# The second layer's memory keys and values, made at the end of the recurrent layer instead of at the start

## The chip, the cores and the metric

The kernel runs on one core of one Trainium2 chip, in one launch. The metric is device time in microseconds (us), the median of several runs. Each run can also be recorded by the hardware profiler; every line of the profile below comes from one such execution of the kernel before. Engines: PE is TensorE (PEld its weight loads), DVE VectorE, ACT ScalarE, POOL GpSimd, SP SyncE, which here only issues transfers.

## The reference, cut to what matters

Two layers over 512 frames of width 1024. Layer 0 mixes by a recurrence (12 heads of 64) and, beside it, by attention into 256 memory tokens (4 heads); layer 1 by chunked attention and, beside it, by memory attention with its own keys and values of the same normalised memory.

```python
def memory_attention(q_mem, mem_n, w_mem_kv):
    k_m, v_m = jnp.split(mem_n @ w_mem_kv, 2, axis=-1)
    ...
    s = jnp.einsum('bshd,bmhd->bhsm', q, k).astype(jnp.float32) * HEAD_DIM ** -0.5
    p = jax.nn.softmax(s, axis=-1).astype(v.dtype)
    return jnp.einsum('bhsm,bmhd->bshd', p, v).reshape(bsz, seq, D_MEMQ)

mem_n = rms_norm(mem, mem_norm)
for layer in range(DEPTH):
    h = rms_norm(x, ln1[layer])
    ...
    mo = memory_attention(q_mem, mem_n, w_mem_kv[layer])
    x = x + jnp.concatenate([mix, mo], axis=-1) @ w_out[layer]
    x = x + conv_glu(rms_norm(x, ln2[layer]), ffn_in[layer], ffn_conv[layer],
                     ffn_conv_b[layer], ffn_out[layer])
return rms_norm(x, ln_f)
```

The keys and values of layer 1 depend on the memory and on the weights alone, so they may be made anywhere ahead of layer 1's attention.

## The kernel before, in words

Everything is fp32 with the features on the partitions. A product is split: each operand into a rounded high half and a low half (`fp32r`), and `dense` does three matmuls per block of 128 features: high by high (L198), high by the activation's low (L199), and, after all of those, the weight's low by high (L202). A weight is loaded by SP into one of two `wraw` buffers, ACT casts it to its high half (L169), and the low half is made either by DVE (L175) or, where `lo_on` is set (the recurrent part), by an ACT copy with the sign turned (L172) on which a POOL transfer adds the weight once more from memory.

The order of the work in the program's text is made by `weave`: each piece of work is a generator that yields planned costs; the one that is furthest behind its share goes next, a pair `(cost, wait)` holds it back in planned time, and a callable holds it until a condition is true. A scheduler then gives each engine its own queue, worked off in order: an instruction that waits holds up all behind it.

The recurrent layer goes by six pairs of heads. `prepare` makes a pair's projections, decays and norms; `front` makes its chunk products and solves a triangular system of 31 dependent steps on DVE (L661 to L668; its right side comes and its result `Xs` goes through memory: `Lr<-d`, `d<-Xs` at L671, `Tt<-d` at L674); `back` turns the solve's result `Tt` into products (transposes L775 on DVE; L780, L788, L794, L804, L815, L821 on PE, ACT's copies between), runs the recurrence over eight chunks (L835 on PE, L836 on DVE, L840 on PE, seven dependent steps), normalises y (L549, a root in small DVE steps, L558), and scales it (L856 to L867).

Before the first pairs, one `weave` interleaves `prepare(0)` with `mem_kv`, which makes keys and values of both layers (L518 the keys' scaling, L528 to L530 the values' three matmuls) and stores the second layer's in `kv1`. The memory is split by `scaled_split` (L238 on ACT, L239 on DVE; in the start's own copy L475 and L476), its norm stands in `macc`. The last `weave` holds `back` of pair 4, `front` and `back` of pair 5, a chain of the layer's memory queries (`q_mem`, L878), the mixed tiles fetched back (`flush_mix`) and the memory attention `mA` (scores L921, maxima L269, exponentials L273, sums' reciprocal L275, division L278, turns L286, values L296), and `ahead`, which starts two tiles of the output projection. After it the x tiles are loaded (L951) and `out_proj` adds them (L333).

Of the kernel before, what the change touches and what calls it, by code (L numbers as in the profile page):

```python
# [111 lines left out]
def trunk_kernel(ctx, tc, A, out):  # L112
# [211 lines left out]
    def out_proj(l, act, gain, h_, l_, xT, order, pre=(), done=()):  # L324
        for m in range(KD):
# [7 lines left out]
            V.tensor_tensor(xT[:, m], xT[:, m], ps[:], op=ALU.add)  # L333
# [106 lines left out]
    mrc = lp.tile([P, 4], F32, name="mrc")  # L440

# [69 lines left out]
    def mem_kv():  # L511
        for l in range(2):
            km, vm_ = (kmT0, vm0) if l == 0 else (tmp(F32, (P, 2, 256)) for _ in range(2))
            for f in range(2):
                w = load_w(A["w_memk"][l, f])
                ps = ps_l()
                yield from dense(ps[:, :NMEM], [(w, K8)], pair_of(mh, ml))
                V.tensor_tensor(km[:, f], ps[:, :NMEM], macc[:, NMEM:], op=ALU.mult)  # L518
            ps = [ps_l(), ps_l()]
            for u in range(2):  # L520
                wh, wl = load_w(A["w_memv"][l, u])
                for j in range(4):
                    k = u * 4 + j
                    for t in range(2):
                        ws = slice(j * 256, (j + 1) * 256)
                        ts = slice(t * P, (t + 1) * P)
                        pt = ps[t][:, :256]
                        PE.matmul(pt, mh[:, k, ts], wh[:, ws], start=k == 0, stop=False)  # L528
                        PE.matmul(pt, ml[:, k, ts], wh[:, ws], start=False, stop=False)
                        PE.matmul(pt, mh[:, k, ts], wl[:, ws], start=False, stop=k == 7)  # L530
                    yield 650
            for t in range(2):
                SC.activation(vm_[:, t], ps[t][:, :256], AF.Copy, scale=mrc[:, t:t + 1])
            if l:
                nc.sync.dma_start(kv1[0], km)
                nc.sync.dma_start(kv1[1], vm_)

    MEMKV_COST = 2 * (16 * 648 + 8 * 650) + 600
# [228 lines left out]
    def back(i, T, dst, tiles=own_tiles, go=None):  # L767
# [57 lines left out]

        psc = bank((P, 8, 64))
# [45 lines left out]

    def q_mem(src, act, qm):
# [53 lines left out]
    def told(g, n):  # L927
        yield from g
        over.add(n)

    def ahead():
        yield lambda: "mem" in over and "state" in Ts[NPAIR - 1]
        yield from out_ahead(0, act1, AHEAD, 2, pre)

# [342 lines left out]
```

## Time and profile before

| | us |
|---|---|
| median of 3 runs | 1379.11 (1378.86 to 1379.75) |
| profiled execution, its own time | 1377.77 |
| span in that profile | 1376.0 |
| mean granted TensorE clock | 0.987 |
| PE busy | 1319.7 (96% of the span) |
| DVE busy | 826.9 (60%) |
| ACT busy | 611.6 (44%) |
| POOL busy | 34.1 (2%) |

A row of the timeline has the start, the length, the engine, the line of the code, the operation with what it writes and reads, and in brackets the idle time of the engine ahead of it with what ended it. Consecutive like instructions share a row (x9). A row of windows gives the stretch and its length, then each engine's busy time with its count in brackets, then the granted clock, the transfers' share and GB/s. A row of groups has the busy time, the mean length of one in ns, and the idle time ahead of them.

### The profile page before, as it was taken

How to read it: one execution, taken by the hardware profiler on the slowest of the kernel's cores; microseconds unless marked ns; L12 is line 12 of the kernel's file. 1: busy time of each engine (PE TensorE's matmuls, PEld its weight loads, DVE VectorE, ACT ScalarE, POOL GpSimd, SP SyncE). 2: the span in 40 equal slices, each digit the busy share in tenths (PEclk: the TensorE clock that was granted, in tenths of full speed). 3: DMA queues.
4: the chain of work that ended last, by engine and by line, in shares of the span. 5: the costliest groups of instructions: out<-in, count | busy, mean ns of one | idle time of the engine just before them, and what ended most of it. 6: DMA issues, size and time to landing. Idle time of an engine off the chain costs nothing. (4 is left out here: it accounts for less than half of the span.)

```text
span 1376.0 us, 20868 instructions
## 1 busy us (share of the span) xinstructions
PE 1319.7 (96%) x8266; PEld 1071.2 (78%) x8266; DVE 826.9 (60%) x1752; ACT 611.6 (44%) x1022; POOL 34.1 (2%) x55
## 2 busy tenths in 40 slices
PE   6999999995999999999999999999999999999996
PEld 5777777774688888888888878786788888888886
DVE  7876789774666555565333667657665565563324
ACT  5556555552444333333222566657443333332321
POOL 3000000000000000000000000000000000000000
PEclk9999999997999999999999999999999999999998
DMA  5276544451042223223232422223223222222332
GB/s 181 83 208 136 109 108 110 99 142 42 24 146 92 92 94 106 92 93 102 84 98 85 152 91 74 90 92 99 93 92 103 96 93 102 98 88 85 104 94 75
DMA packets 63506, 139.18 MB, mean 101 GB/s; under 512 B 24624, under 2 KB 28336, under 8 KB 63408
## 3 DMA queue, kind: packets, MB, share of 16 engines
q1 hardware_dynamic: 60672, 127.89, 29.3%
q0 software_dynamic: 2736, 9.96, 4.2%
q8 instruction: 65, 1.06, 0.3%
q14 instruction: 33, 0.27, 0.1%
HBM read 131.01 MB, written 6.82 MB: 100 GB/s over the span
## 5 line engine op out<-in xcount | busy, mean ns | idle before, releaser
L175 DVE TENSOR_TENSOR wlo<-wraw,whi 128x1024 fp32r<-128x1024 f32 x183 | 218.9, 1197 | 128.4 <-PE psd L202 118.3
L169 ACT CAST whi<-wraw 128x1024 fp32r<-128x1024 f32 (+1 forms) x202 | 207.6, 1029 | 153.3 <-PE psd L199 38.5
L198 PE MATMUL psd<-r1h,whi 128*128 128x512 f32 x336 | 136.6, 407 | 1.3 <-ACT whi L169 1.2
L198 PE MATMUL psf<-r2h,whi 128*128 128x512 f32 x352 | 137.2, 390 | 0.0
L198 PE MATMUL psf<-r1h,whi 128*128 128x512 f32 x352 | 137.2, 390 | 0.0
L199 PE MATMUL psf<-r1l,whi 128*128 128x512 f32 x352 | 137.1, 390 | 0.0
L199 PE MATMUL psf<-r2l,whi 128*128 128x512 f32 x352 | 137.1, 390 | 0.0
L199 PE MATMUL psd<-r1l,whi 128*128 128x512 f32 x336 | 134.1, 399 | 0.0
L202 PE MATMUL psd<-r1h,wlo 128*128 128x512 f32 x336 | 92.5, 403 | 3.1 <-DMA wlo<-in_wA_dram 3.1
L199 PE MATMUL psd<-f3l,whi 128*128 128x512 f32 (+1 forms) x238 | 88.7, 377 | 0.0
L198 PE MATMUL psd<-f3h,whi 128*128 128x512 f32 (+1 forms) x238 | 88.6, 377 | 0.0
L358 DVE TENSOR_TENSOR tmp<-psf,rho 128x512 f32<-128x512 f32 x44 | 30.4, 692 | 94.7 <-PE psf L202 94.7
L202 PE MATMUL psf<-r1h,wlo 128*128 128x512 f32 x352 | 87.0, 389 | 0.0
L202 PE MATMUL psf<-r2h,wlo 128*128 128x512 f32 x352 | 86.9, 389 | 0.0
L198 PE MATMUL psd<-r2h,whi 128*128 128x512 f32 (+1 forms) x200 | 77.6, 392 | 0.1
L198 PEld LDWEIGHTS psd<-r1h,whi 128*128 128x128 f32 x336 | 63.8, 190 | 17.4 <-issue 2.4
L199 PE MATMUL psd<-r2l,whi 128*128 128x512 f32 (+1 forms) x200 | 76.4, 385 | 0.8 <-DVE r2l L215 0.8
L202 PEld LDWEIGHTS psf<-r1h,wlo 128*128 128x128 f32 x352 | 66.1, 188 | 13.7
L202 PEld LDWEIGHTS psf<-r2h,wlo 128*128 128x128 f32 x352 | 66.1, 188 | 13.7
L199 PEld LDWEIGHTS psf<-r1l,whi 128*128 128x128 f32 x352 | 66.1, 188 | 13.6
L198 PEld LDWEIGHTS psf<-r2h,whi 128*128 128x128 f32 x352 | 66.1, 188 | 13.7
L199 PEld LDWEIGHTS psf<-r2l,whi 128*128 128x128 f32 x352 | 66.1, 188 | 13.6
(352 smaller groups left out, 2429.2 us busy)
## 6 DMA issues: line engine op xcount, KB each, us to landing
wraw<-in_ffn_in_dram SPq DMA_DIRECT2D x88, 512.0 KB, 3.3
wraw<-in_ffn_out_dram SPq DMA_DIRECT2D x32, 448.0 KB, 3.3
wraw<-in_wA_dram SPq DMA_DIRECT2D x20, 512.0 KB, 4.3
wlo<-in_wA_dram POOLq DMA_DIRECT2D x17, 512.0 KB, 7.7
wraw<-in_w_out_dram SPq DMA_DIRECT2D x16, 512.0 KB, 3.8
wraw<-in_ffn_out_dram SPq DMA_DIRECT2D x16, 512.0 KB, 4.1
wraw<-in_wB_dram SPq DMA_DIRECT2D x8, 512.0 KB, 3.4
Lr<-d SPq DMA_DIRECT2D x24, 128.0 KB, 5.5
```

The source lines that it names most:

```text
L169: SC.copy(hi[:, :n], raw)
L175: V.tensor_tensor(lo[:, :n], raw, hi[:, :n], op=ALU.subtract)
L198: PE.matmul(ps, wh[:, j * P:(j + 1) * P], ah, start=start and n == 0, stop=False)
L199: PE.matmul(ps, wh[:, j * P:(j + 1) * P], al, start=False, stop=False)
L202: PE.matmul(ps, wl[:, j * P:(j + 1) * P], act(k)[0], start=False, stop=stop and n == len(ks) - 1)
L358: V.tensor_tensor(v[:], pv[:], rho[:], op=ALU.mult)
```

## The change

`mem_kv` now makes one layer per call, in banks that are passed in, with weights requested one ahead, the values' high products first and low ones after, and smaller planned costs. The first `weave` makes layer 0 alone. In the last `weave` a new chain does the memory queries, then `mem_again`, then `flush_mix`: `mem_again` loads the memory once more through the two `wraw` buffers, splits it into tiles of `r1h` and `r1l` that `flush_mix` fills later, and calls `mem_kv(1, ...)`, with the low halves by POOL. The memory attention has its own place in the `weave`, from the queries on. The last pair's `back` holds its recurrence until "kv" is in `over`; between its `front` and `back` a planned wait of 25000 ns is put. `ahead` loads two x tiles into a `wraw` buffer, and `out_proj` adds them from there. Line numbers in the changed file are 11 higher in the recurrent part, 13 in the later part of `back`, 15 to 17 in the memory's.

```diff
-    def out_proj(l, act, gain, h_, l_, xT, order, pre=(), done=()):
+    def out_proj(l, act, gain, h_, l_, xT, order, pre=(), done=(), early=None):
...
-            V.tensor_tensor(xT[:, m], xT[:, m], ps[:], op=ALU.add)
+            was = early[:, m * S:(m + 1) * S] if early is not None and m < 2 else xT[:, m]
+            V.tensor_tensor(xT[:, m], was, ps[:], op=ALU.add)
...
+    mrho = lp.tile([P, NMEM], F32, name="mrho")
...
-    def mem_kv():
-        for l in range(2):
-            km, vm_ = (kmT0, vm0) if l == 0 else (tmp(F32, (P, 2, 256)) for _ in range(2))
-            for f in range(2):
-                w = load_w(A["w_memk"][l, f])
-                ps = ps_l()
-                yield from dense(ps[:, :NMEM], [(w, K8)], pair_of(mh, ml))
-                V.tensor_tensor(km[:, f], ps[:, :NMEM], macc[:, NMEM:], op=ALU.mult)
...
-    MEMKV_COST = 2 * (16 * 648 + 8 * 650) + 600
+    def mem_kv(l, mh, ml, mrho, bank):
+        km, vm_ = (kmT0, vm0) if l == 0 else (tmp(F32, (P, 2, 256)) for _ in range(2))
+        srcs = [A["w_memk"][l, 0], A["w_memk"][l, 1], A["w_memv"][l, 0], A["w_memv"][l, 1]]
+        sent = [load_w(srcs.pop(0))]
+
+        def take_w():
+            if srcs:
+                sent.append(load_w(srcs.pop(0)))
+            return sent.pop(0)
+
+        for f in range(2):
+            w = take_w()
+            ps = bank()
+            for y in dense(ps[:, :NMEM], [(w, K8)], pair_of(mh, ml)):
+                yield y / 2
+            V.tensor_tensor(km[:, f], ps[:, :NMEM], mrho, op=ALU.mult)
+        ps = [bank(), bank()]
+        for u in range(2):
+            wh, wl = take_w()
...
+            for k, t, ws, ts in at:
+                PE.matmul(ps[t][:, :256], mh[:, k, ts], wh[:, ws], start=k == 0, stop=False)
+                PE.matmul(ps[t][:, :256], ml[:, k, ts], wh[:, ws], start=False, stop=False)
+                if t:
+                    yield 480
+            for k, t, ws, ts in at:
+                PE.matmul(ps[t][:, :256], mh[:, k, ts], wl[:, ws], start=False, stop=k == 7)
+                if t:
+                    yield 240
...
+    MEMKV_COST = 8 * 648 + 8 * 720
...
+        if go is not None:
+            yield lambda: "kv" in over
         psc = bank((P, 8, 64))
         psy = bank((P, 8, 64))
...
-    weave([(first, .981 * PREP_COST), (chain(lora_one(), mem_kv()), 16 * 648 + MEMKV_COST)])
+    V.tensor_copy(mrho[:], macc[:, NMEM:])
+    weave([(first, .981 * PREP_COST), (chain(lora_one(), mem_kv(0, mh, ml, mrho[:], ps_l)), 16 * 648 + MEMKV_COST)])
...
+    def q_there():
+        yield lambda: "q" in over
+
+    def later(ns):
+        yield 0, ns
...
-        yield lambda: "mem" in over and "state" in Ts[NPAIR - 1]
+        yield lambda: "mem" in over and "flush" in over and "state" in Ts[NPAIR - 1]
         yield from out_ahead(0, act1, AHEAD, 2, pre)
+        early.append(wp.tile([P, 1024], F32, name="wraw", tag="wraw", bufs=2))
+        nc.sync.dma_start(early[0][:], A["xT"][:, 0:2].rearrange("p a b -> p (a b)"))
...
+    def mem_again():
+        h4, l4 = (t[:, 0:4].rearrange("p a (b m) -> p (a b) m", b=2) for t in (r1h, r1l))
+        for u in range(2):
+            raw = wp.tile([P, 1024], F32, name="wraw", tag="wraw", bufs=2)
+            nc.sync.dma_start(raw[:], A["memT"][:, 4 * u:4 * u + 4].rearrange("p a b -> p (a b)"))
+            for j in range(4):
+                scaled_split(raw[:, j * NMEM:(j + 1) * NMEM], 4 * u + j, "mem_norm", h4, l4)
+        yield 0, 2000
+        yield from mem_kv(1, h4, l4, mrho[:], ps_d)
+        over.add("kv")
     a_, b_ = NPAIR - 2, NPAIR - 1
     weave([(told(back(a_, Ts[a_], dst_mix), "back"), 1.5 * BACK_COST),
-           (chain(front(b_, Ts[b_]), back(b_, Ts[b_], dst_mix, other_tiles, lambda: "back" in over)),
+           (chain(front(b_, Ts[b_]), later(25000), back(b_, Ts[b_], dst_mix, other_tiles, lambda: "back" in over)),
             1.5 * (FRONT_COST + BACK_COST)),
-           (told(chain(q_mem(lambda f: A["wA"][18 + f], hact, qmA), flush_mix(), mA), "mem"),
-            16 * 648 + mem_cost(860)),
+           (told(chain(q_mem(lambda f: A["wA"][18 + f], hact, qmA), mem_again(), flush_mix()), "flush"),
+            16 * 648 + MEMKV_COST),
+           (told(chain(q_there(), mA), "mem"), mem_cost(860)),
            (ahead(), 14 * 648)], tc)
...
-    for m in range(0, KD, 2):
+    for m in range(2, KD, 2):
         nc.sync.dma_start(xT[:, m:m + 2], A["xT"][:, m:m + 2])
```

On DVE, in the last pair's solve (the products `Xu<-Lr,Xs` and sums `Xs<-Xs,Xu` alternate), before:

```order
L666 TENSOR_TENSOR Xu<-Lr,Xs 128x48
L878 SCALAR_TENSOR_TENSOR kh<-psd,rho 128x512
L668 TENSOR_TENSOR Xs<-Xs,Xu 128x6x8
L215 TENSOR_TENSOR r1l<-tmp,r1h 128x512
L666 TENSOR_TENSOR Xu<-Lr,Xs 128x49
L215 TENSOR_TENSOR r1l<-tmp,r1h 128x512
L668 TENSOR_TENSOR Xs<-Xs,Xu 128x7x7
L175 TENSOR_TENSOR wlo<-wraw,whi 128x1024
```

and in the changed kernel at the same steps:

```order
L677 TENSOR_TENSOR Xu<-Lr,Xs 128x48
L239 SCALAR_TENSOR_TENSOR r1l<-wraw,vec,r1h 128x256
L679 TENSOR_TENSOR Xs<-Xs,Xu 128x6x8
L239 SCALAR_TENSOR_TENSOR r1l<-wraw,vec,r1h 128x256
L677 TENSOR_TENSOR Xu<-Lr,Xs 128x49
L239 SCALAR_TENSOR_TENSOR r1l<-wraw,vec,r1h 128x256
L679 TENSOR_TENSOR Xs<-Xs,Xu 128x7x7
L239 SCALAR_TENSOR_TENSOR r1l<-wraw,vec,r1h 128x256
L677 TENSOR_TENSOR Xu<-Lr,Xs 128x42
L239 SCALAR_TENSOR_TENSOR r1l<-wraw,vec,r1h 128x256
L679 TENSOR_TENSOR Xs<-Xs,Xu 128x7x6
L269 TENSOR_REDUCE mst<-pss 128x2
```

The splits of the fetched tiles and of a weight (L215, L175) gave place to the splits of the reloaded memory (L239) and, further on, to the memory attention's maxima (L269).

On PE, at the last pair's first products (`AR,ML`; the row's second name is what is read), before:

```order
L202 MATMUL psd<-r1h,wlo 128x512 x2
L780 MATMUL pss<-AR,ML 32x32 [waits DVE_49,PE_49]
L788 MATMUL pss<-VT,ML 64x64 [waits PE_49]
L788 MATMUL pss<-VT,ML 64x64 x11
L780 MATMUL pss<-AR,ML 32x32 [waits DVE_49]
L780 MATMUL pss<-AR,ML 32x32 x14
L788 MATMUL pss<-VT,ML 64x64 x4
L804 MATMUL pss<-VT,Tt_93 64x128 [waits PE_49]
```

and in the changed kernel (L198, L199, L202 with 256 columns are the second layer's keys, L848 and L853 pair 4's recurrence):

```order
L199 MATMUL psd<-r1l,whi 128x256
L198 MATMUL psd<-r1h,whi 128x256
L199 MATMUL psd<-r1l,whi 128x256
L202 MATMUL psd<-r1h,wlo 128x256 [waits DMASW1_49]
L202 MATMUL psd<-r1h,wlo 128x256
L848 MATMUL psl<-W,MQ 64x64 [waits DVE_49]
L848 MATMUL psl<-W,MQ 64x64
L853 MATMUL psl<-MQ,W 64x64 x2
L202 MATMUL psd<-r1h,wlo 128x256 x2
L791 MATMUL pss<-AR,ML 32x32 [waits DVE_49]
L799 MATMUL pss<-VT,ML 64x64 [waits PE_49]
L799 MATMUL pss<-VT,ML 64x64 x10
```

The last pair's first product (L780, now L791) stood behind the memory queries; it now stands behind the first keys' low products, which wait for POOL's transfer (DMASW).

On SP, around the solve's round trip, before:

```order
L180 DMA wraw<-in_w_out_dram 128x1024 [waits DMAHW4_49,DMAHW6_49,DVE_49,Activation_49]
L671 DMA d_3723<-Xs 256x1x32 [waits DVE_49]
L671 DMA d_3723<-Xs 256x1x32 [waits DMAHW0_49]
L671 DMA d_3723<-Xs 256x1x32 [waits DMAHW1_49]
L671 DMA d_3723<-Xs 256x1x32 [waits DMAHW2_49]
L674 DMA Tt_94<-d_3723 32x8x32 [waits DMAHW3_49,DMAHW2_49,DMAHW7_49,DMAHW1_49,DMAHW0_49]
L674 DMA Tt_94<-d_3723 32x8x32
```

and in the changed kernel:

```order
L180 DMA wraw<-in_w_memk_dram 128x1024 [waits DMAHW3_49,DVE_49]
L682 DMA d_3593<-Xs 256x1x32 [waits DMAHW4_49,DVE_49]
L682 DMA d_3593<-Xs 256x1x32 [waits DMAHW5_49]
L682 DMA d_3593<-Xs 256x1x32 [waits DMAHW6_49]
L682 DMA d_3593<-Xs 256x1x32 [waits DMAHW7_49]
L180 DMA wraw<-in_w_memv_dram 128x1024 [waits DMAHW2_49,DMAHW0_49,Activation_49]
L685 DMA Tt_94<-d_3593 32x8x32 [waits DMAHW6_49,DMAHW5_49,DMAHW7_49,DMAHW4_49,DMAHW1_49]
L685 DMA Tt_94<-d_3593 32x8x32
L685 DMA Tt_94<-d_3593 32x8x32 [waits DMAHW3_49]
```

A load of the second layer's value weights, which waits for ACT, now stands between the store of the solve's result and its reload.

31 lines of the change are left out of this document (11 added, 20 removed).

## The prediction

> **What bounds the kernel now.** I read the span in windows first, then PE's waits, then the timeline around the one wait that stands out. The change touches two places: the start, where both layers' memory keys and values are made, and the end of the recurrent layer, where it puts the second layer's. The windows (columns: length with PE's busy time, then PEld, DVE, ACT, POOL, each with its count; then granted clock, DMA share, GB/s):
>
> ```profile
> 60.00:70.00 10.00, 9.82 (x93) 8.37 (x92) 8.79 (x18) 5.40 (x10) 0.00 (x0) 1.00 0.27 68
> ...
> 80.00:90.00 10.00, 10.00 (x81) 8.98 (x81) 8.03 (x22) 4.72 (x5) 0.22 (x1) 1.00 0.40 149
> ...
> 310.00:315.00 5.00, 1.69 (x20) 0.84 (x18) 4.69 (x17) 2.21 (x5) 0.00 (x0) 0.89 0.61 109
> 315.00:320.00 5.00, 0.00 (x0) 0.00 (x0) 4.62 (x17) 0.00 (x0) 0.00 (x0) 0.50 0.28 92
> 320.00:325.00 5.00, 0.00 (x0) 0.00 (x0) 0.35 (x2) 0.30 (x1) 0.00 (x0) 0.50 0.21 41
> 325.00:330.00 5.00, 3.62 (x74) 3.41 (x76) 0.87 (x2) 0.80 (x3) 0.00 (x0) 0.50 0.17 26
> ```
>
> At the start PE is full in both windows, so a matmul taken from there should shorten the span; DVE stands at 8 to 9 of 10 beside it. At the layer's end PE is nearly empty from 310 to 325 us while DVE is full until 320. The waits and PE's own line say what for:
>
> ```profile
> PE psd L202 <- DMA wlo<-in_wA_dram: 3.1, 1, 3.1
> ...
> PE pss L780 <- DVE AR L775: 14.7, 1, 14.7
> ...
> 295.02 0.66 PE L558 MATMUL pss<-cst,tmp 128*128 128x128 f32 x4 [0.15 <-DVE tmp L555]
> ...
> 326.38 0.28 PE L780 MATMUL pss<-AR,ML 32*32 32x32 f32 x2 [14.69 <-DVE AR L775]
> ...
> 380.41 0.50 PE L198 MATMUL psd<-r1h,whi 128*128 128x512 f32 x1
> ```
>
> The wait is for the last pair's 31-step solve on DVE and the two DMA round trips behind it:
>
> ```profile
> 311.85 0.26 DVE L666 TENSOR_TENSOR Xu<-Lr,Xs 128x60 f32<-128x60 f32 x1
> ...
> 312.40 0.24 DVE L666 TENSOR_TENSOR Xu<-Lr,Xs 128x54 f32<-128x54 f32 x1
> 312.56 0.68 DVE L215 TENSOR_TENSOR r1l<-tmp,r1h 128x512 fp32r<-128x512 f32 x1
> ...
> 313.89 0.22 DVE L666 TENSOR_TENSOR Xu<-Lr,Xs 128x48 f32<-128x48 f32 x1
> ...
> 316.26 1.23 DVE L175 TENSOR_TENSOR wlo<-wraw,whi 128x1024 fp32r<-128x1024 f32 x1
> ...
> 319.88 0.17 DVE L668 TENSOR_TENSOR Xs<-Xs,Xu 128x8 f32<-128x8 f32 x1
> ...
> 320.08 2.52 SPq L671 DMA_DIRECT2D d<-Xs  x4
> 324.09 1.82 SPq L674 DMA_DIRECT2D Tt<-d  x4
> ```
>
> So the stage from L558 at 295.02 to the first matmul of the output projection's third tile at 380.41 lasts 85.4 us; I call 295.02 zero. The solve ends at +25.0, the last pair's chain starts at +31.4, 6.4 later.
>
> **The change part by part.** Front. One layer is 96 matmuls of 256 columns (16 key and 16 value steps, three products each). Their pitch:
>
> ```profile
> 67.57 0.28 PE L528 MATMUL psl<-whi,ML 128*128 128x256 f32 x1
> ...
> 72.22 0.28 PE L530 MATMUL psl<-wlo,ML 128*128 128x256 f32 x1
> ```
>
> The second row is 41 matmuls after the first: 0.113 us each, 96 make 10.9 us. With them go four weight splits on DVE (L175) and two scalings (L518), which helps the solve beside them. Bounds of the gain: 11.1 (all of it and the 0.2 of a matmul's end) and 8 (the 3.1 us wait for a low half reopens in full earlier, since less work stands ahead of it). I take 10.0, nearer the first, because PE was full in both windows: **−10.0**. It falls below 8 only if DVE, at 8.79 of 10, sets this stage once PE has less.
>
> Ahead of the end stage's zero the changed order has nine more 512-column matmuls (the memory queries'), which leave the stage itself:
>
> ```profile
> 305.44 0.40 PE L199 MATMUL psd<-r1l,whi 128*128 128x512 f32 x1
> ...
> 308.66 0.39 PE L199 MATMUL psd<-r1l,whi 128*128 128x512 f32 x1
> ```
>
> Fourteen pitches in 3.22 us, 0.23 each: **+2.1** there.
>
> The solve. Inserted work costs its length less what hides between dependent steps: the pair of steps from 311.85 to 312.40 took 0.55, the next, with two L215 in it, 1.49 (to 313.89), so two of 0.68 cost 0.94, about 0.22 less than their length apiece. The new inserts have these lengths:
>
> ```profile
> L476 DVE SCALAR_TENSOR_TENSOR ML<-VT,vec,ML 128x256 fp32r<-128x256 f32 x8 | 4.7, 600 | 0.0
> ...
> L269 DVE TENSOR_REDUCE mst<-pss 128x2 f32<-128x512 f32 x8 | 5.5, 687 | 1.2 <-PE pss L921 1.2
> ...
> L278 DVE TENSOR_SCALAR krv<-krv,mst 128x256 f32<-128x256 f32 x8 | 2.5, 349 | 0.1
> ...
> L816 DVE TENSOR_TENSOR MQ<-pss,cst 128x256 f32<-128x256 f32 x2 | 0.8, 424 | 8.3 <-PE pss L815 8.3
> ...
> L836 DVE SCALAR_TENSOR_TENSOR W<-psl,dE,VT 128x64 f32<-128x64 f32 x6 | 1.7, 280 | 0.8 <-PE psl L835 0.8
> ```
>
> Less 0.22 each: four sums into MQ at L816's length 0.8, one 128x512 product and one query scaling at L215's length 0.9, eight splits of the reloaded memory at L476's mean 3.0, four reductions 1.9, six divisions (L278) 0.8: 7.4; out go four L215, one L175 and one query scaling at L215's length, 3.3. I take 3 of the difference of 4.1, since a mean of 600 over eight in 4.7 us may hold waiting, and 2 for a later start of the solve behind the transposes and norms of the pair before: solve end +30.0. Bounds +27 (only half of either) and +32.
>
> The chain behind it. In the new order of SP a load of second-layer value weights stands between the solve's store and its reload, and on PE the low half of the first key weights stands ahead of the last pair's first product. That half is a POOL transfer added onto ACT's copy, whose landing is seen here:
>
> ```profile
> L169 ACT CAST whi<-wraw 128x1024 fp32r<-128x1024 f32 (+1 forms) x202 | 207.6, 1029 | 153.3 <-PE psd L199 38.5
> ...
> wraw<-in_w_out_dram SPq DMA_DIRECT2D x3, 512.0 KB, 3.7
> ...
> wlo<-in_w_out_dram POOLq DMA_DIRECT2D x1, 512.0 KB, 8.2
> ```
>
> ACT's pair of copies at 1.03 each stands about where the solve ends, so the second is there 2.2 behind it; the transfer lands 8.2 later, at +40.4, and PE starts the pair's chain after four low matmuls and one recurrence step (0.86 below), at **+41.7** against +31.4. Bound from below: the half is there first and only the solve counts, +36.4. The Trainium skill, "DMA: Bandwidth & Descriptors", fits such a software transfer as 2.0 us plus bytes over 436e3 per us, 3.2 us for 512 KB; by that the chain would start at +36.7, but the transfer of 512 KB here took 8.2, and the row decides.
>
> What follows it, by these rows:
>
> ```profile
> L921 PE MATMUL pss<-kmT,kh 64*128 64x256 f32 x16 | 4.8, 409 | 0.0
> ...
> L296 PE MATMUL pss<-KB,vm 128*64 128x512 f32 x12 | 4.1, 613 | 0.0
> ...
> L286 PE MATMUL pss<-cst,krv 128*128 128x128 f32 x16 | 2.7, 290 | 0.0
> ...
> 345.50 0.33 PE L835 MATMUL psl<-W,MQ 64*64 64x64 f32 x4
> ...
> 345.88 0.28 DVE L836 SCALAR_TENSOR_TENSOR W<-psl,dE,VT 128x64 f32<-128x64 f32 x1 [0.47 <-PE psl L835]
> ...
> 356.58 1.05 PE L549 MATMUL pss<-cst,tmp 128*128 128x2 f32 x8
> ...
> 371.23 0.81 ACT L857 ACTIVATE tmp<-tmp,vec 128x512 f32<-128x512 f32 x1
> ```
>
> The pair's small products, four groups of sixteen with ACT's copies between, an estimate from the same steps at full clock: 7.2. Then 73 matmuls of the second layer (8.3), eight records of scores (2.4), 30 of sums (3.9 at the pitch, 5.1 by the row), six of probabilities times values (2.1), norms 1.2: 17.9. The recurrence waits until the keys and values are done ("kv"): evacuation and its first products 2.2, then seven steps; one is 0.38 until DVE starts (345.50 to 345.88), 0.28 there and an estimated 0.2 back, 0.86, 6.0 for seven, and DVE's splits between them (one at L175's 1.23, two at L215's 0.68, by the order) 2.6 to 2.8: 8.8. Before, these steps lay among the memory attention; now **nothing is left to cover them**. Tail: 27 matmuls ahead (6.2), the square sums (1.0), a dozen dependent small DVE steps for the root at the solve's 0.27 (3.3), the L558 group (0.7), then y's scaling, three DVE steps at L215's length and two of ACT at L857's, in which PE stands (3.7), and ACT's copy and square ahead of all (1.6): 16.5. Sum 41.7 + 7.2 + 17.9 + 2.2 + 8.8 + 16.5 = 94.3, **+8.9** against 85.4.
>
> x early. The two x tiles were not waited for, so their early load gains nothing; but they hold a weight buffer until the output projection adds them, and a load of its weights waits for that on SP: **+1.0**, between 0 (hidden) and 3.7 (a whole load).
>
> Clock. After a stop PE runs slower for a while; the same six matmuls after a stop of 3.1 us, and without one:
>
> ```profile
> 99.76 2.79 PE L202 MATMUL psd<-r1h,wlo 128*128 128x512 f32 x6
> ...
> 308.89 1.52 PE L202 MATMUL psd<-r1h,wlo 128*128 128x512 f32 x6
> ```
>
> 1.27 each; two stops of about 3 us, at the low half and in the tail, **+2.5**; bounds 0 (the old stop had a slow time too, granted clock 0.50 from 325 to 330, which the steps above, at full clock, leave out) and 4 (three stops). The Trainium skill, "TensorE: Matmul & The Clock Gate", Part 1, gives the half rate after an idle window of about 3.4 us; by it both stops would cost nothing, whereas the row at 99.76 shows a cost after 3.1.
>
> Sum: −10.0 + 2.1 + 8.9 + 1.0 + 2.5 = **+4.5**, from the profiled execution's own 1377.77 to 1382.3. The median of the three runs, 1379.11, lies 1.3 above that execution: **1383.6**.
>
> **The rivals.** (1) *The hole is filled*: PE's 14.7 us take the moved work, the low half lands before PE reaches it and the solve ends at +27: chain at +33.4, end at 33.4 + 52.6 = 86.0, +0.6; no new stop. −10.0 + 2.1 + 0.6 + 1.0 = −6.3: 1372.8. For it: 15 us of empty PE and 11 us of work. Against: that work needs splits from the DVE which makes the hole. (2) *Even*: the chain starts at +38, between the bounds, and one stop less is paid for the clock: −10.0 + 2.1 + 5.2 + 1.0 + 1.3 = −0.4, 1378.7. For it: ACT's copy needs no place behind the solve; against: its queue. (3) *The low halves come one after another*: four transfers of 8 us, two weight buffers, each waiting for ACT's copy; where the next three are also late by 2 us each, the stage grows 6 more: 1389.6. It decides once PE reaches a low half earlier than about 12 us after its load's issue. That the change does not do what it says (the front is DVE's, the gain 4) ends near there too.
>
> **How the numbers follow.** Changes under 0.2% (2.8 us) can't be told from none here. Forecast 0.39, own range 1380 to 1388; filled hole 0.28; even 0.18; late halves or lost front 0.15. The first and fourth are slower, 0.54; faster 0.28; same 0.18. The range leaves a tenth on each side: 1371 to 1392.
>
> **What would show it.** Right: 60:90 closes by about 10 us; the first wait of PE after the solve is on a low half of key weights, not on AR; recurrence steps alone at 0.86; stage near 94. Wrong if the stage stays below 89 us, if PE has no stop over 2 us in it, or if the front gives under 8.

## The result and the profile after

The changed kernel takes 1394.61 us (median of 4 runs, 1388.67 to 1396.23) against 1379.43 for the kernel before in the same runs: ratio 1.0102, 95% interval 1.0071 to 1.0132. It was forecast slower, at 1383.6 and at most 1392; it lies 11 us above the forecast. The profiled execution took 1396.23 (span 1394.5, mean granted clock 0.978). It is the slowest of the four, so the two profiles, whose spans differ by 18.5 us, show 3 us more than the medians, which differ by 15.2.

Two marks split the difference. The first is the last pair's spread product, four matmuls of `prepare` that spread the root of a norm (L558 before, L569 after), at which the prediction set its zero; the second is the first product of the channel mixer (`psf`, L198). Behind the second little differs: 962.8 us remain before, 963.8 after. PE's timeline of the changed kernel at both marks, and then of the kernel before at the second:

```profile
295.79 0.60 PE L569 MATMUL pss<-cst,tmp 128*128 128x128 f32 x4
...
430.67 0.39 PE L198 MATMUL psf<-r2h,whi 128*128 128x512 f32 x1
```

```profile
413.18 0.39 PE L198 MATMUL psf<-r2h,whi 128*128 128x512 f32 x1
```

Up to the first mark the changed kernel gained nothing in this execution: 295.79 against 295.02. From mark to mark it takes 134.9 us against 118.2, which is +16.7. PE's waits in the changed kernel, 60 to 300 us and then 296 to 432 (engine, tile and line, what it waited for; total, times, longest):

```profile
PE pss L791 <- DVE Tl L786: 5.8, 5, 2.6
PE pss L569 <- DVE Xs L679: 3.8, 3, 1.7
PE pss L826 <- ACT W L816: 2.2, 3, 1.0
PE psl L843 <- issue: 1.7, 1, 1.7
PE psd L202 <- DMA wlo<-in_wA_dram: 1.2, 1, 1.2
```

```profile
PE pss L286 <- DVE Xu L677: 5.7, 1, 5.7
PE psd L848 <- DVE AR L849: 5.2, 5, 3.6
PE psd L198 <- ACT r1h L214: 3.6, 1, 3.6
```

The wait of 14.7 us is gone. In its place stand 5.7 us in the last pair's solve, 5.2 in its recurrence and 3.6 in the tail; ahead of the first mark there are now several stops of 1 to 2.6 us, most of them at the pairs' spread products (L569) and first products (L791), where the kernel before had none over 1.3 past 100 us. The windows show what follows such stops (columns as before: PE, PEld, DVE, ACT, POOL, granted clock, DMA share, GB/s):

```profile
80.00:90.00 10.00, 8.76 (x49) 6.74 (x48) 9.43 (x34) 7.80 (x12) 1.73 (x2) 1.00 0.84 185
...
115.00:120.00 5.00, 3.23 (x56) 2.61 (x58) 2.43 (x5) 2.10 (x5) 0.00 (x0) 0.89 0.65 201
120.00:125.00 5.00, 5.00 (x57) 3.79 (x53) 1.99 (x3) 3.17 (x8) 0.00 (x0) 0.50 0.06 26
...
255.00:260.00 5.00, 4.18 (x46) 3.05 (x48) 2.19 (x5) 1.78 (x4) 0.00 (x0) 0.55 0.46 167
260.00:265.00 5.00, 5.00 (x83) 4.27 (x81) 4.38 (x15) 3.73 (x9) 0.00 (x0) 0.77 0.00 0
...
320.00:325.00 5.00, 1.39 (x6) 1.07 (x7) 5.00 (x23) 4.04 (x17) 0.00 (x0) 0.53 0.47 160
325.00:330.00 5.00, 5.00 (x14) 3.44 (x14) 2.45 (x9) 4.54 (x9) 0.86 (x1) 0.50 0.48 52
330.00:335.00 5.00, 5.00 (x19) 2.65 (x17) 1.90 (x8) 4.83 (x10) 0.86 (x1) 0.60 0.92 191
...
375.00:380.00 5.00, 4.48 (x33) 3.41 (x34) 2.02 (x5) 1.91 (x4) 0.00 (x0) 0.50 0.01 4
```

Two things are to be seen. From 80 to 90 us DVE is now at 9.43 of 10 and PE at 8.76: PE no longer sets this part alone. And PE is "busy" 5.00 of 5.00 at a granted clock of 0.50 or 0.60, after the longer stops: busy, but at half rate.

An account of PE's time between 60 us and the first mark puts this together. "Idle" is the sum of the gaps between PE's rows; "half rate" is, over windows of 2.5 us, PE's busy time times one less the granted clock; the rest is work at full rate. The figures of the account are of one profiled execution each, medians and ratios of the timed runs.

| kernel | median | ratio to before in its runs | first mark | work | idle | half rate | mark to mark |
|---|---|---|---|---|---|---|---|
| before | 1379.4 | 1 | 295.0 | 223.5 | 9.9 | 1.7 | 118.2 |
| changed | 1394.6 | 1.0102 | 295.8 | 211.2 | 16.4 | 8.2 | 134.9 |
| front_new | 1380.9 | 1.0014 | 291.7 | 211.3 | 14.8 | 5.6 | 123.9 |
| front_old | 1371.8 | 0.9967 | 284.7 | 207.6 | 14.1 | 3.0 | 118.9 |
| front_none | 1377.1 | 0.9991 | 287.7 | 198.6 | 21.1 | 8.0 | 122.9 |
| cost_only | 1379.0 | 1.0004 | 295.9 | 221.9 | 11.6 | 2.4 | 117.8 |
| end_only | 1398.2 | 1.0141 | 294.4 | 223.6 | 9.1 | 1.7 | 136.2 |
| old_loops | 1404.7 | 1.0176 | 305.9 | 206.9 | 20.1 | 18.9 | 134.1 |
| no_early_x | 1396.1 | 1.0130 | 291.0 | 211.7 | 15.9 | 3.4 | 138.3 |
| no_gate | 1393.1 | 1.0104 | 295.1 | 210.5 | 16.1 | 8.5 | 133.8 |
| no_split | 1387.6 | 1.0068 | 290.9 | 209.4 | 14.9 | 6.6 | 132.5 |
| heat_pairs | 1398.2 | 1.0153 | 295.9 | 217.2 | 12.1 | 6.5 | 139.0 |
| heat_end | 1395.6 | 1.0132 | 296.6 | 210.7 | 17.7 | 8.2 | 136.3 |
| fp32_kv | 1389.3 | 1.0097 | 294.0 | 211.4 | 17.7 | 4.9 | 131.9 |
| fp32_old | 1400.2 | 1.0172 | 300.1 | 207.8 | 20.7 | 11.6 | 131.9 |
| free | 1412.3 | 1.0253 | 289.6 | 211.5 | 14.7 | 3.4 | 156.3 |

The changed kernel sheds 12.3 us of work ahead of the first mark, and 6.5 of idle time and 6.5 of half rate take all of it back. (By count of products it is 8.8: 10.9 gone, 2.1 of queries more. The other 3.5 the account does not resolve, so its figures are good to a few us.)

How much comes back is in part luck of the execution. Up to 300 us no_early_x, no_gate, no_split, heat_end and free have the changed kernel's instructions on PE, DVE and ACT in the same order. So the table holds six executions of one front: the first mark comes at 289.6 to 296.6, 293.2 on average, with 14.7 to 17.7 us idle and 3.4 to 8.5 at half rate. The idle time is there in each; the half rate varies, and 295.8 is one of the later marks.

From mark to mark the same account gives work 99.5 before and 108.3 after, idle 16.4 and 16.5, half rate 2.3 and 10.1. The 16.7 us are thus 8.8 of work, which is the moved products (10.9) less the queries (2.1), and 7.8 of half rate. PE stands idle as long as before: the hole was broken up, not filled.

### The profile page after: what moved, and what is told of

It is laid out like the page before. It is cut to its first block, busy times and chain, and to the rows that moved or that the text cites. A ratio compares the mean times of both kernels' runs of the same rounds, so it can differ in the third digit from the quotient of the medians.

```text
span 1394.5 us, 20898 instructions
## 1 busy us (share of the span) xinstructions
PE 1330.5 (95%) x8266; PEld 1081.4 (78%) x8266; DVE 823.5 (59%) x1757; ACT 619.0 (44%) x1034; POOL 37.3 (3%) x59
## 5 line engine op out<-in xcount | busy, mean ns | idle before, releaser
L175 DVE TENSOR_TENSOR wlo<-wraw,whi 128x1024 fp32r<-128x1024 f32 (+1 forms) x179 | 214.1, 1196 | 131.7 <-PE psd L202 119.0
L198 PE MATMUL psd<-r1h,whi 128*128 128x512 f32 (+1 forms) x352 | 142.7, 406 | 4.7 <-ACT r1h L214 3.6
L199 PE MATMUL psd<-r1l,whi 128*128 128x512 f32 (+1 forms) x352 | 140.0, 399 | 0.2 <-DVE r1l L215 0.2
L198 PE MATMUL psf<-r2h,whi 128*128 128x512 f32 x352 | 137.1, 390 | 0.0
L198 PE MATMUL psf<-r1h,whi 128*128 128x512 f32 x352 | 137.1, 390 | 0.0
L199 PE MATMUL psf<-r2l,whi 128*128 128x512 f32 x352 | 137.0, 389 | 0.0
L199 PE MATMUL psf<-r1l,whi 128*128 128x512 f32 x352 | 136.9, 389 | 0.0
L202 PE MATMUL psd<-r1h,wlo 128*128 128x512 f32 (+1 forms) x352 | 97.1, 402 | 1.2 <-DMA wlo<-in_wA_dram 1.2
L199 PE MATMUL psd<-f3l,whi 128*128 128x512 f32 (+1 forms) x238 | 88.6, 377 | 0.0
L198 PE MATMUL psd<-f3h,whi 128*128 128x512 f32 (+1 forms) x238 | 88.5, 376 | 0.0
L202 PE MATMUL psf<-r2h,wlo 128*128 128x512 f32 x352 | 87.0, 389 | 0.0
L202 PE MATMUL psf<-r1h,wlo 128*128 128x512 f32 x352 | 86.9, 389 | 0.0
L198 PEld LDWEIGHTS psd<-r1h,whi 128*128 128x128 f32 x352 | 68.6, 195 | 22.6 <-ACT r1h L214 3.9
L199 PEld LDWEIGHTS psd<-r1l,whi 128*128 128x128 f32 x352 | 68.6, 195 | 14.1 <-issue 0.8
L198 PE MATMUL psd<-r2h,whi 128*128 128x512 f32 (+1 forms) x200 | 77.5, 391 | 0.1
L199 PE MATMUL psd<-r2l,whi 128*128 128x512 f32 (+1 forms) x200 | 76.3, 384 | 0.8 <-DVE r2l L215 0.8
L202 PEld LDWEIGHTS psf<-r2h,wlo 128*128 128x128 f32 x352 | 66.1, 188 | 13.8
L198 PEld LDWEIGHTS psf<-r1h,whi 128*128 128x128 f32 x352 | 66.1, 188 | 13.7
L202 PEld LDWEIGHTS psf<-r1h,wlo 128*128 128x128 f32 x352 | 66.1, 188 | 13.7
L198 PEld LDWEIGHTS psf<-r2h,whi 128*128 128x128 f32 x352 | 66.1, 188 | 13.7
```

What stands on the lines that cost most here:

```text
L175: V.tensor_tensor(lo[:, :n], raw, hi[:, :n], op=ALU.subtract)
L198: PE.matmul(ps, wh[:, j * P:(j + 1) * P], ah, start=start and n == 0, stop=False)
L199: PE.matmul(ps, wh[:, j * P:(j + 1) * P], al, start=False, stop=False)
L202: PE.matmul(ps, wl[:, j * P:(j + 1) * P], act(k)[0], start=False, stop=stop and n == len(ks) - 1)
```

## The experiments

**The front alone.** Two kernels take only the removal from the kernel before, so they leave out the second layer's keys and values; one has the new loops, one the old. The first, with its new `mem_kv` left out here:

```diff
...
-    weave([(first, .981 * PREP_COST), (chain(lora_one(), mem_kv()), 16 * 648 + MEMKV_COST)])
+    V.tensor_copy(mrho[:], macc[:, NMEM:])
+    weave([(first, .981 * PREP_COST), (chain(lora_one(), mem_kv(0, mh, ml, mrho[:], ps_l)), 16 * 648 + MEMKV_COST)])
+    nc.sync.dma_start(kv1[0], kmT0[:])
+    nc.sync.dma_start(kv1[1], vm0[:])
```

> The kernel before with the new mem_kv in the first weave for layer 0 alone; the second layer's keys and values are left out (kv1 holds the first layer's), the end of the recurrent layer is as before. Theory A (the pairs' chains between 115 and 295 us take back whatever the front gives): 12 us are ahead at 115 us, but L558 of the last pair (295.02 before) comes at 292 to 295 and the time falls by 0 to 3 us, 1376 to 1379. Theory B (the front's gain is real and is lost in the changed kernel only because its instruction order in the later pairs came out worse): L558 at 284 to 288, 1368 to 1372.

```diff
-        for l in range(2):
+        for l in range(1):
...
+            nc.sync.dma_start(kv1[0], kmT0[:])
+            nc.sync.dma_start(kv1[1], vm0[:])
...
-    MEMKV_COST = 2 * (16 * 648 + 8 * 650) + 600
+    MEMKV_COST = (16 * 648 + 8 * 650) + 300
```

> The same with the old loops of mem_kv, run for layer 0 only, so the same work is left out but another instruction order results. Theory A: the same 0 to 3 us gain as with the new loops, within 1.5 us of it. Theory B: a gain of its own, anywhere from 2 to 11 us, that differs from the new loops' by more than 3 us.

front_new takes 1380.85 us against 1378.10 before (ratio 1.0014, 1.0003 to 1.0024): 11 us of PE work less, and not faster. front_old takes 1371.75 (0.9967, 0.9949 to 0.9985), with runs from 1368.09 to 1378.64. They differ by 9.1 us, so theory A as written falls, and the gain of 10 does arrive at the first mark in one order (284.7, in the second fastest of its ten executions; their median is 3.4 us slower). But neither is B whole: front_new has no bad end order to blame, and still only 3.3 of its gain reach the first mark.

**Is the front PE's at all?** A third kernel makes neither layer there.

```diff
-        for l in range(2):
+        for l in range(0):
...
+        V.memset(kmT0[:], 0.0)
+        V.memset(vm0[:], 0.0)
+        nc.sync.dma_start(kv1[0], kmT0[:])
+        nc.sync.dma_start(kv1[1], vm0[:])
```

> The kernel before with neither layer's keys and values made in the first weave (both left out, zeros take their place), the old code otherwise: 22 us of PE work less at the front. If the front and the pairs behind it are bound by PE, another 10 us go beyond what leaving one layer out gave in the best order (1371.75): 1360 to 1363, the last L558 at 273 to 277. If the pairs' own chain on DVE and through memory is the floor once one layer is gone, the second layer's removal turns into stops: the last L558 at 281 to 287, PE idle between 60 us and it above 18 us, 1368 to 1374.

It takes 1377.09 us, 0.9991 (0.9974 to 1.0008) of before: twice the work removed, and no gain that can be told. The place where it stops longest ahead of the first mark is pair 0's first product, on PE's timeline of front_none:

```profile
114.16 0.28 PE L786 MATMUL pss<-Tl,ML 32*32 32x32 f32 x2 [8.84 <-DVE Tl L781]
```

PE stands there for 8.84 us, waiting for the transposes of the first solve's result. The same product in the kernel before, in front_old and in the changed kernel:

```profile
120.83 0.69 PE L780 MATMUL pss<-Tl,ML 32*32 32x32 f32 x32
```

```profile
112.63 0.22 PE L779 MATMUL pss<-Tl,ML 32*32 32x32 f32 x2 [0.43 <-DVE Tl L774]
```

```profile
113.56 0.21 PE L791 MATMUL pss<-Tl,ML 32*32 32x32 f32 x2 [0.65 <-DVE Tl L786]
```

Before it came at 120.83 without a wait; in these three it comes at 112.6 to 114.2, whatever is removed. The solve's last step on DVE, before, after, in front_none and in old_loops (below), shows what it waits for:

```profile
106.03 0.18 DVE L668 TENSOR_TENSOR Xs<-Xs,Xu 128x8 f32<-128x8 f32 x1
```

```profile
100.99 0.17 DVE L679 TENSOR_TENSOR Xs<-Xs,Xu 128x8 f32<-128x8 f32 x1
```

```profile
101.69 0.17 DVE L674 TENSOR_TENSOR Xs<-Xs,Xu 128x8 f32<-128x8 f32 x1
```

```profile
108.94 0.17 DVE L703 TENSOR_TENSOR Xs<-Xs,Xu 128x8 f32<-128x8 f32 x1
```

It moves by 5.0 us in the changed kernel and no further with two layers gone; with one layer gone it also ends at 102.15 (front_old), 105.14 (front_new) and 108.94 (old_loops). So the pair's chain, on DVE and through memory, is the floor of the first weave, and how early it ends depends on the order of DVE's instructions, not only on the work taken from PE. In the orders tried some 7 to 8 of the 10.9 us can be had there (120.83 to 113.56 or 112.63), less what later pairs add. The last pair's L558 (287.7) lies just above what the floor's theory expected (281 to 287), and the idle time (21.1) above its bound of 18, as expected. The time, 1377.1, is worse than its 1368 to 1374: half rate takes 8.0 ahead of the first mark, and mark to mark the kernel is 4.7 longer than before.

**Order without work.** The new planned cost alone, in the kernel before:

```diff
-    MEMKV_COST = 2 * (16 * 648 + 8 * 650) + 600
+    MEMKV_COST = 2 * (8 * 648 + 8 * 720) + 600
```

> The kernel before with the new planned cost for the memory's work (2 x (8 x 648 + 8 x 720) + 600 instead of 2 x (16 x 648 + 8 x 650) + 600) and nothing else: the same instructions, in a slightly other order. If order alone moves this kernel by several us, it differs from 1378 to 1379 by more than 2 us either way; if it does not, it is within 1.5.

1379.01 us, 1.0004 (0.9994 to 1.0013): no change. In the kernel before, with both layers at the front, this other order costs nothing.

**The end alone.** The changed kernel, with the front as before, so that the second layer's keys and values are made twice:

```diff
...
-    weave([(first, .981 * PREP_COST), (chain(lora_one(), mem_kv(0, mh, ml, mrho[:], ps_l)), 16 * 648 + MEMKV_COST)])
+    weave([(first, .981 * PREP_COST), (chain(lora_one(), mem_kv_both()), 16 * 648 + MEMKV_BOTH)])
```

> The changed kernel, but the first weave makes both layers' keys and values in the old way too (11 us of PE work done twice). Theory A: what the end costs is all that is seen, the last L569 near 295 to 297 and the stage after it 100 to 104 us: 1395 to 1399, no worse than the changed kernel by more than 3 us. Theory B: the front's 11 us come on top of the changed kernel: 1400 to 1407.

1398.20 us, 1.0141 (1.0126 to 1.0156). Its first mark is that of the kernel before (294.4), its mark to mark 136.2, +18.0. The end costs that by itself, and the front gives the changed kernel some 4 to 5 of it back (1398.2 against 1394.6; ratios 1.0141 and 1.0102), not 10.

**The old loops at the front of the changed kernel.**

```diff
...
-    weave([(first, .981 * PREP_COST), (chain(lora_one(), mem_kv(0, mh, ml, mrho[:], ps_l)), 16 * 648 + MEMKV_COST)])
+    weave([(first, .981 * PREP_COST), (chain(lora_one(), mem_kv_first()), 16 * 648 + (16 * 648 + 8 * 650) + 300)])
```

> The whole change, but layer 0's keys and values in the first weave are made by the old loops with their old planned costs. The two kernels that left the second layer out differed by 9 us (1380.85 with the new loops, 1371.75 with the old ones). Theory B1 (the new loops' order in the first weave is what lost the front's 10 us): the last L569 comes at 284 to 288 instead of 295.8 and the time is 1384 to 1388. Theory A1 (whatever order, the later pairs take it back once the end is changed too): L569 at 291 to 296, 1391 to 1396.

1404.66 us, 1.0176 (1.0139 to 1.0212): both expectations missed, and the first mark moved 10 us the wrong way, to 305.9. The old loops are no better as such: the same loops gave 284.7 in front_old. The first solve ends 6.8 us later here (108.94 against 102.15), PE stops of 1.6 to 2.8 us follow in most pairs, and the account gives idle 20.1, half rate 18.9. The windows of old_loops behind a stop of 2.72 us at pair 0's first product:

```profile
120.00:125.00 5.00, 3.37 (x47) 3.05 (x48) 1.56 (x3) 0.07 (x2) 0.86 (x1) 0.61 1.00 214
125.00:130.00 5.00, 5.00 (x58) 3.81 (x60) 3.07 (x5) 2.76 (x6) 0.00 (x0) 0.50 0.65 174
130.00:135.00 5.00, 5.00 (x37) 3.44 (x34) 4.12 (x18) 2.64 (x7) 0.00 (x0) 0.50 0.10 30
135.00:140.00 5.00, 5.00 (x58) 4.45 (x56) 2.09 (x7) 3.05 (x8) 0.00 (x0) 0.68 0.00 0
```

One stop of 2.72 us, which ends at 121.63, and PE, full from there on, runs at half rate for some 16 us: twice what the granted clock lacks of 1.00 is 3.9, 5.0, 5.0 and 3.2 us in the four windows.

**Parts of the end.** The early x tiles left out:

```diff
-        early.append(wp.tile([P, 1024], F32, name="wraw", tag="wraw", bufs=2))
-        nc.sync.dma_start(early[0][:], A["xT"][:, 0:2].rearrange("p a b -> p (a b)"))
...
-    for m in range(2, KD, 2):
+    for m in range(0, KD, 2):
...
```

> The changed kernel without the early load of the two x tiles (they are loaded as before). If the buffer that they hold costs the 1 us of the prediction, this is 1 us faster than the changed kernel, 1393 to 1394; if they are hidden, 0; if the early load gained something, slower. The tail's stop of 3.6 us ahead of the output projection stays either way.

1396.06 us, 1.0130 (1.0111 to 1.0147): not faster. Mark to mark it takes 138.3 against 134.9, with a new wait of 2.9 us of PE for the x tiles' sum. The early load is worth some 3 us in that stretch by these two executions, where the prediction charged 1.0 for it; the medians' difference is too small for their intervals. Its front is the changed kernel's: idle 15.9 and 16.4, but half rate 3.4 and 8.2, and the first mark at 291.0 and 295.8.

The recurrence let go ahead of the keys and values:

```diff
-        if go is not None:
-            yield lambda: "kv" in over
```

> The changed kernel without the condition that the last pair's recurrence waits for the second layer's keys and values. The prediction's term: a recurrence with nothing beside it costs 8.8 us and measured 10.3 (367.1 to 377.4). If that is a cost of the gate, the steps move in among the second layer's products and the time falls by 4 to 9 us, 1386 to 1391. If the recurrence is held by its own chain and by the banks it shares, it stays behind the products: within 3 us of 1394.6.

1393.06 us, 1.0104 (1.0082 to 1.0127) against the changed kernel's 1.0102: the condition costs nothing that can be told. With it gone the recurrence lies among other work, but the end comes no earlier.

The low halves of the reloaded memory left out:

```diff
-                scaled_split(raw[:, j * NMEM:(j + 1) * NMEM], 4 * u + j, "mem_norm", h4, l4)
+                SC.activation(h4[:, 4 * u + j], raw[:, j * NMEM:(j + 1) * NMEM], AF.Copy, scale=Vc("mem_norm", 4 * u + j))
```

> The changed kernel without the eight low halves of the reloaded memory on DVE (left out: the low half of the memory in the second layer's keys and values is whatever the tile held). Theory of the sum (the splits cost the solve about 3 us, the rest stays): solve's end 2 to 3 us earlier after the last L569, PE's stop of 5.7 us ahead of L286 falls to 3 or less, time 2 to 4 us lower. Theory of the clock (the stop itself costs less than the half rate that follows it, granted clock 0.52 from 320 to 330): with the stop under 3 us the slow stretch goes too and the time falls by 5 to 9 us.

1387.64 us, 1.0068 (1.0049 to 1.0086), 4.7 us under the changed kernel by the ratios. In the profiled executions 2.4 of it lie mark to mark, with the stop at L286 down from 5.7 to 3.1 and the solve's end at +28.8 instead of +29.4; 4.9 more lie ahead of the first mark, where the program's order is the same, and are not the splits'. The sum's theory holds for the length of the stage but not for the reason that it gave: the solve ends 0.6 earlier and not 2 to 3. The clock's theory is not borne out, since 11.5 us are still lost to half rate in the stage.

Plain fp32 products instead, without splits, casts, low halves and POOL transfers, in the changed kernel and in old_loops:

```diff
-                scaled_split(raw[:, j * NMEM:(j + 1) * NMEM], 4 * u + j, "mem_norm", h4, l4)
+                SC.activation(mf[u][:, j], raws[u][:, j * NMEM:(j + 1) * NMEM], AF.Copy, scale=Vc("mem_norm", 4 * u + j))
...
-        yield from mem_kv(1, h4, l4, mrho[:], ps_d)
...
+                PE.matmul(ps[:, :NMEM], w[:, k * P:(k + 1) * P], mf[k // 4][:, k % 4], start=k == 0, stop=k == 7)
...
+                    PE.matmul(ps[t][:, :256], mf[u][:, j, t * P:(t + 1) * P], w[:, j * 256:(j + 1) * 256], start=k == 0, stop=k == 7)
```

> The changed kernel with the second layer's keys and values made as plain fp32 products from unsplit operands: no split of the memory on DVE, no ACT cast, no low halves, no POOL transfers, 32 products of 256 columns instead of 96; no weight load stands between the solve's store and its reload. If the end's 17 to 18 us come from what the splits and the low halves hold up, the stage falls from 134.9 to 122 to 127 and the time to 1380 to 1387. If they come from the recurrence behind the kv condition and the tail, it stays above 130.

> The same end with layer 0's keys and values by the old loops. The stage as in fp32_kv within 3 us; the front depends on the order that comes out: the last L569 anywhere from 285 (as without the second layer) to 306 (as with the old loops and the whole change). Where it is near 285, the time is 1372 to 1380 and near or below the kernel before.

1389.32 us, 1.0097 (1.0067 to 1.0127), and 1400.21, 1.0172 (1.0154 to 1.0191). Mark to mark 131.9 in both, 3.0 under the changed kernel and not the 8 to 13 expected. But this swaps work as well: the 32 plain products stand as 64 records and keep PE busy for some 20 us, in part at half rate, where the 96 that they replace take 10.9 by their pitch (groups of fp32_kv from 294 to 426 us),

```profile
L983 PE MATMUL psd<-wlo,wraw 128*128 128x256 f32 x32 | 11.0, 443 | 0.0
L993 PE MATMUL psd<-wraw,wlo 128*128 128x256 f32 x32 | 9.1, 430 | 0.0
```

and by the account work rises by 3.2 (111.5 against 108.3), while idle time falls by 5.5 (11.0) and half rate by 0.7 (9.4). So the splits and the low halves hold up some 6 of the 16.7, and 9.4 of half rate stay without them. fp32_old again shows the front of old_loops (300.1, half rate 11.6).

Neither the planned wait nor the condition:

```diff
-        if go is not None:
-            yield lambda: "kv" in over
...
-           (chain(front(b_, Ts[b_]), later(25000), back(b_, Ts[b_], dst_mix, other_tiles, lambda: "back" in over)),
+           (chain(front(b_, Ts[b_]), back(b_, Ts[b_], dst_mix, other_tiles, lambda: "back" in over)),
```

> The changed kernel without the planned wait of 25000 ns and without the kv condition: the last pair's first product now stands ahead of the second layer's products on PE, which lie beside its chain and its recurrence. If the end's 16.7 us come mostly from that order (chain start 12.5 us later), PE's long stop comes back (8 to 14 us), the chain starts at 31 to 36 after the last L569 and the stage falls from 134.9 to 126 to 131. If the products' own 11 us and DVE set it, the stage stays at 132 to 137.

1412.34 us, 1.0253 (1.0219 to 1.0287), the slowest of all: mark to mark 156.3. PE's waits of free from 290 us on:

```profile
PE pss L791 <- DVE AR L786: 26.0, 1, 26.0
PE psd L198 <- ACT r1h L214: 7.1, 2, 4.0
```

With the last pair's first product ahead of the memory's products on PE, everything waits 26.0 us behind it, and all of that work comes afterwards. Both expectations missed; the place of this one product is worth 20 us, and the changed kernel's is the better one.

**Products to keep the clock.** Idle products (fp32, 128x512) whose results are not used: two per pair ahead of the first products of pairs 0 to 4, or six ahead of the first L286:

```diff
+        if go is None:
+            for _ in range(2):
+                PE.matmul(ps[:], C("ident"), cst[:, 0:S], start=True, stop=True)
```

> The changed kernel with two idle products (fp32, 128x512, some 0.9 us each, written to the bank that the real ones fill next) ahead of each pair's first L791 product, pairs 0 to 4. In the changed kernel PE stops there for up to 2.6 us, and the granted clock then falls: 8.5 us worth of full rate is lost to it between 60 and 300 us, against 1.7 in the kernel before. Theory of the clock (it is the half rate behind short stops that ate the front's gain): the stops close, at most 4 us are lost between 60 and 300, the last L569 comes 2 to 6 us earlier than the 291 to 296 seen with this order, though ten products more are done. Rival (the chains hold the pairs, the clock only follows): the last L569 comes later by what the products cost, up to 9 us, 296 to 303.

```diff
+                if l == 0 and f == 0 and hh == 0 and kt == 0:
+                    for _ in range(6):
+                        PE.matmul(ps[:], C("ident"), cst[:, 0:S], start=True, stop=True)
```

> The changed kernel with six such products ahead of the first L286, where PE stops for 5.7 us in the last pair's solve and runs at 0.52 and 0.80 in the 20 us after it. Theory of the clock: the stop shrinks below 1 us, the granted clock stays above 0.9 from 310 to 340, and the stage from the last L569 to the first ffn product (134.9 us, or 133 to 136 with its neighbours) falls by 3 to 6. Rival (PE does not set the end there, DVE does): the clock stays up, and the stage changes by less than 2.

heat_pairs takes 1398.2 us, 1.0153 (1.0136 to 1.0170). Work rose by 6.0 and idle fell by 4.3 up to the first mark, which stands at 295.9: the products went into stops, but they did not bring the gain, since the half rate between pairs 0 and 1 stayed (6.5). With the first mark of the changed kernel's front anywhere from 289.6 to 296.6, this decides nothing between the two theories. Mark to mark, where the last two of them lie (some 1.8 us), it takes 139.0, 4.1 more than the changed kernel; what makes up the rest is not shown. In heat_end (1395.58 us, 1.0132, 1.0109 to 1.0155) the products waited for their bank and ran behind the stop, not in it, on PE's timeline of heat_end:

```profile
322.87 7.11 PE L286 MATMUL pss<-cst 128*128 128x512 f32 x12 [4.12 <-ACT krv L273]
```

So the kernel does not do what it was meant to. It still tells something: 7.1 us of useless products end at 329.98, the real ones start 5.4 us later than in the changed kernel (33.2 us after the first mark instead of 27.8), and yet the last pair's chain starts at +44.2 against +43.9. From the first real L286 to the chain's start the same 68 matmuls take 11.0 us here and 16.0 in the changed kernel: the 5 us came back because the work then ran at full rate. That is what the slow stretch behind the stop costs there.

No version that was tried and computes everything beats the kernel before.

## Why the prediction was wrong

The direction and the place of the loss were right, the size was not, and the step that failed is the first term of the sum. The clock's term, much too small, comes second.

**Front, "I take 10.0, nearer the first, because PE was full in both windows".** This failed. It bounded the loss by one wait of 3.1 us. With the 2.1 of the early queries −7.9 was forecast for the first mark, and +0.8 came; over the six executions of this front it is +1.6 to −5.4, −1.8 on average. PE was full there, but it was not alone: the prediction's own escape, DVE at 8.79 of 10, was the case. front_none shows it: with two layers gone the first pair's solve ends no earlier (101.69) than with one in the changed kernel (100.99), and PE stands for 8.84 us. PE's spare products had been the cover of the pairs' chains; without them it arrives first and waits in most pairs. The account above gives the sizes.

**The end, +8.9 with +1.0 and +2.5 beside it, 12.4 in all.** At the prediction's own mark, the third output tile's first product, it is +17.0 (398.17 less 295.79 is 102.4, against 85.4). Its steps, each from the first mark: solve's end +30.0 forecast, +29.4 measured; chain start +41.7 and +43.9. The chain's start comes near its place, but not for the reason given. DVE's last row of the solve in the changed kernel, and the rows of PE's timeline at the chain's start and at the third tile:

```profile
325.00 0.17 DVE L679 TENSOR_TENSOR Xs<-Xs,Xu 128x8 f32<-128x8 f32 x1
```

```profile
338.50 0.40 PE L202 MATMUL psd<-r1h,wlo 128*128 128x256 f32 x2
...
339.64 0.24 PE L791 MATMUL pss<-AR,ML 32*32 32x32 f32 x2
...
398.17 0.63 PE L198 MATMUL psd<-r1h,whi 128*128 128x512 f32 x1
```

The low half's product has no wait in front of it. POOL's transfer did take its time (a median of 8.6 us), but PE came later still: 5.7 us of stop at L286 and the half rate behind it had already eaten the time. Then chain to recurrence 27.3 forecast, 28.5 measured; recurrence 8.8 and 9.7; tail 16.5 and 20.3, of which about 3.2 is half rate (granted clock 0.84 over these 20.3 us). The recurrence has a stop that the sum named only in part, on PE's and DVE's timelines of the changed kernel:

```profile
374.83 0.48 PE L848 MATMUL psd<-AR,Lr 64*64 64x64 f32 x4 [3.62 <-DVE AR L849]
```

```profile
373.88 0.69 DVE L215 TENSOR_TENSOR r1l<-tmp,r1h 128x512 fp32r<-128x512 f32 x1 [3.18 <-ACT r1h L214]
374.50 0.28 DVE L849 SCALAR_TENSOR_TENSOR AR<-psd,dE,VT 128x64 f32<-128x64 f32 x1
```

DVE's step of the recurrence stands behind the split of a fetched tile, which waits for ACT's half of it. The claim that nothing covers the recurrence was right, but lifting the condition (no_gate) moved the recurrence among other work and brought nothing, so the end does not pay for it as such.

**Early x, +1.0.** Wrong in sign: about −3, by the one wait that no_early_x shows.

**Clock, +2.5 for two stops.** Too small. 10.1 us of PE's busy time are lost to half rate mark to mark against 2.3 before, though part of it in places where PE does not set the end; at L286 alone it costs 5 (heat_end). And the pairs, for which the sum had no clock term, lost 8.2, and 3.4 to 8.5 over the six executions, against 1.7 before.

With the six executions' average the front falls 6.1 us short of its forecast and the end 4.6, together the 10.7 by which the medians' difference exceeds the forecast of +4.5. The end's figure is of one execution, so a match that close is partly luck.

**The rivals.** The filled hole (1372.8) did not come: 5.7 us of it stayed at L286, and with the new stops behind it PE's idle time mark to mark is what it was (16.4 and 16.5). Late low halves in turn did not come either; no low product of the second layer waited. The lost front, put beside that rival at a gain of 4, is what happened, with an end 4.6 dearer than forecast.

What stays open is why one order keeps the front's gain (front_old, 284.7) and the next loses all of it. The end of the first solve (102.15 there, 100.99 to 108.94 elsewhere) is one part. Which stop is followed by how long a slow stretch differs between executions of the same program, so the orders' differences cannot be put down to single instructions here.

## What to carry to other kernels

A full engine is not proof that work taken from it shortens the span: look for the engine beside it that would be next, and ask which chains this work was covering. Work that is moved into a hole brings its splits, casts and loads along, and these fall on the engine that made the hole; count them on that engine first. And where the granted clock falls after stops, several new stops can cost more than one long one: here the half rate behind the long stop fell mostly on an empty stretch (2.3 us lost), that behind the shorter ones on work (10.1). Before a difference of a few us between two profiles is explained, find out how far two executions of one order lie apart; here it was 7 us at one mark.

## What the hardware showed that was not expected

Stops far shorter than the 14.7 us of before lowered the granted clock: 2.72 us brought some 16 us at half rate in old_loops, 2.61 us brought 0.55 and 0.77 over ten in the changed kernel, and 1.91 us there, which ended at 116.77, brought 0.50 over 120 to 125. Its stop of 1.67 us, which ended at 274.67, was followed by no fall, and neither was one of 2.35 us in no_early_x (granted clock 1.00 from 270 to 280), so the length of the stop alone does not decide. The Trainium skill, "TensorE: Matmul & The Clock Gate", Part 1, gives an idle window of about 3.4 us for the half rate and as long a busy one for the way back; here 1.9 to 2.7 us sufficed and the way back took up to 16 us of full PE. The changed kernel's front in no_early_x differed by 4.8 us at the first mark (295.8 and 291.0) with idle time equal within 0.5: the whole difference lay in the clock.
